# Encoder trunk on one core: weight sums issued by a budget, two small moves in the order

## The chip, the cores and the metric

The kernel runs on one core of a Trainium2 chip (trn2). The metric is the device time of one execution in microseconds. A core has TensorE (PE; its weight loads are shown apart as PEld), VectorE (DVE), ScalarE (ACT), GpSimd (POOL), and SyncE (SP), which here only issues DMAs.

## The reference

One layer of an encoder, batch 1, 512 tokens of width 1024, all float32:

```
x += [hgrn2 heads ; mlstm heads](rmsnorm(x) @ w_in + b_in) @ w_out
x += cross_attention(rmsnorm(x), rmsnorm(mem))       # 4 heads, 256 memory tokens: w_xq, w_xkv, w_xo
x += square(relu(rmsnorm(x) @ w_up)) @ w_down        # 1024 -> 4096 -> 1024
return rmsnorm(x)
```

Both groups of recurrent heads (four and four, of width 128) run a forward and a backward scan.

## The kernel before, in words

**Products.** Weights lie in DRAM as blocks of 128x1024 float32 (512 KB), in the order of use (`wpk`, `SEQ`). A block is loaded by SP into a tile `st` (three buffers), and split in two: ScalarE rounds it into `wh`, VectorE writes the rest, `st - wh`, into `wl` (`split_out`, L342; three buffers each). The activations are split in the same way. A product is then three matmuls per piece: high by high, high by low, low by high (L346 to L348, L1305 to L1307, L1588 to L1590). `weights` (L277) splits the block in use and the next two, and loads the fourth. So the split of block n writes over the buffers of block n-3, and waits until TensorE is done with that.

**Stages.** In this order: the input projection with the recurrent heads beside it (SEQ 0 to 36), K and V of the memory (37 to 52), the mixer's output projection (53 to 60), the query projection with the attention heads beside it (61 to 68), the cross-attention's output projection, and the MLP in four quarters of an up stage and a down stage each (st 0 to 7).

**Seven products for eight.** The cross-attention's output projection and the MLP's stages do a two by two block product with seven products, P1 to P7, each in two parts, a and b (`JOBS` L1161, `MORDER` L1215). P1 to P3 use plain weight blocks; P4 to P7 use sums of blocks, and activations that are sums too ("forms", made in `up`, L1540: `first` makes the P5 form, `second` the P6 form, `by_p3` and `by_p7` the others). The order of the MLP's products on TensorE is written out by hand.

**Sums of weights.** `make_forms` (L304) builds the MLP's weight sums in DRAM, beside the earlier stages: `start` and `follow` are plain copies issued by SP, `add` is an accumulating DMA issued by POOL. It is a generator of 88 steps, 44 copies and 44 adds of 512 KB each. `next_form` (L248) takes one step; a copy is put behind the last weight load in SP's order, an add waits for the last split that VectorE has made. `weights` takes a step for each block from SEQ 6 on, and a second one at every third (L283). That is 84 steps by the end of the query projection. The last four are taken in the MLP (L1280). The sums of the cross-attention's output projection are made in SBUF by other DMAs on POOL (`sum_loads`, `add_block` L1179; tiles `as` and `gate`); the MLP's down stages also add in SBUF (`sum_add`, tile `as`).

**The order elsewhere** is set by a scheduler that follows the program, with `tc.high_priority()` lifting what stands in it. In `up`, the weight splits and the readings of PSUM stand in it; the squares (`square`, L1545: ReLU, then square, on ScalarE) don't.

**The gates.** `gates_chain` (L708) makes the mLSTM decay terms: two scans on VectorE over the rows (L782, twice), two more that need a row mask (L786, twice; the mask is loaded at L768), and a subtraction (L813), after which ScalarE copies the result (L815).

Of the kernel before, what the change touches and what calls it, by code (L numbers as in the profile page):

```python
# [80 lines left out]
def trunk(ctx: ExitStack, tc: tile.TileContext, x, mem, wpk, vec, cst, lmask, rmask, rows, out):  # L81
    nc = tc.nc
# [18 lines left out]
    def smb():  # L101
        return pss.tile([P, 512], F32, tag="sm", name=nm("sm"))
# [39 lines left out]
    def behind(a, b):  # L142

        tc.add_manual_dep(a.ins, b.ins.name, mybir.DependencyInfo(mybir.DependencyClass.NoSync, mybir.DependencyReason.DATA),
                          reason="order of an engine")
# [99 lines left out]
    st_tiles, hl_tiles = {}, {}  # L245
    last_load, last_made = [None], [None]

    def next_form():  # L248

        o = next(form_steps, None)  # L250
        if o is not None:
            if o.ins.engine == mybir.EngineType.SP:
                behind(o, last_load[0])
            else:
                after(o, last_made[0])
                accs.append(o)
# [20 lines left out]
    def weights(key):  # L277
        i = SIDX[key]
        with (tc.high_priority() if i > 2 else ExitStack()):
            for n in range(i, i + 3):  # L280
                split(n)
            load(i + 3)
        for _ in range((i >= 6) + (i >= 6 and i % 3 == 0)):  # L283
            next_form()
        return hl_tiles[i]

    mforms = {}
# [52 lines left out]
    form_steps = make_forms()  # L340
# [367 lines left out]
    def gates_chain():  # L708
        grow = ml["grow"]
        ps = smb()  # L710
# [43 lines left out]
        yield  # L754

        lp = A4()
        gp.memset(lp[:, 0:512], 0.0)
        for dr in range(2):
            v.tensor_copy(ap(lp, dr * 32, [P, 4], [1, 4]), ap(lf, dr * 4, [8, 4], [1, 4]))
            v.tensor_copy(ap(lp, 64 + dr * 32, [P, 4], [1, 4]), igd(dr))  # L760
        ps = smb()
# [2 lines left out]
        lrow = grow[:, 512:1024]  # L764
        sc.activation(lrow[0:64, 0:512], ps[0:64, :], AF.Copy)
        sc.activation(grow[0:64, 0:512], ps[64:128, :], AF.Copy)
        rm = lp[:, 512:1024]
        nc.sync.dma_start(out=rm[0:64, 0:512], in_=rmask)  # L768
        yield
        fm = A4()  # L770
        Fr, mr = fm[:, 0:512], fm[:, 512:1024]
# [17 lines left out]
        ps = smb()  # L789
# [195 lines left out]
    for t in range(2):  # L985
# [8 lines left out]
        r, _ = rstd_of(ss, 1, D)  # L994
# [6 lines left out]
    for k in range(8):  # L1001
        ps = smb()
        for t in range(2):
            pe.transpose(ps[:, t * P:t * P + P], mt[t][:, k * P:k * P + P], ident)
        g = vc[:, V_MEM + k:V_MEM + k + 1]
# [155 lines left out]
    JOBS = [(p, g) for p in ("P1", "P7", "P2", "P5", "P6", "P3", "P4") for g in range(2)]  # L1161
# [112 lines left out]
    def mahead(n):  # L1274
        with tc.high_priority():
            for m in range(n, n + 3):
                msplit(m)
            for m in range(n + 3, n + 7):
                mload(m)
        if n % 2 and n >= len(JOBS):  # L1280
            next_form()
        return mhl[n]


# [5 lines left out]
    def by_blocks(st, sta, banks, done, ready=None, after=None):  # L1290

        mlp = st >= 0
        user = {"P1": 0, "P2": 1, "P5": 2, "P6": 0, "P3": 2, "P7": 0 if mlp else 3, "P4": 0}
        opens = {"P1", "P2", "P5"} if mlp else {"P1", "P2", "P5", "P7"}
        jobs = MORDER[st] if mlp else JOBS
        held = {}

        def product(p, g, u, w, first, end):
            for k in range(2):
                ah, al = [t[:, u * P:u * P + P] for t in sta[2 * g + k][p]]  # L1300
                bh, bl = [t[:, k * 512:k * 512 + 512] for t in w]
                new = first and k == 0 and p in opens
                fl = dict(skip_group_check=True)
                ps = held[user[p]][u]
                pe.matmul(ps, lhsT=ah, rhs=bh, start=new, stop=False, **fl)  # L1305
                pe.matmul(ps, lhsT=ah, rhs=bl, start=False, stop=False, **fl)  # L1306
                pe.matmul(ps, lhsT=al, rhs=bh, start=False, stop=end and k == 1, **fl)  # L1307
            if after is not None:
                after()

        def ahead(n):
            if mlp:
                return mahead(len(JOBS) * st + n)
            with tc.high_priority():
                for m in range(n, n + 3):
                    job(m)
                i = max(hl_tiles)
                for m in range(i + 1, i + 4):
                    load(m)
                for m in range(n + 3 - len(JOBS), n + 7 - len(JOBS)):  # L1320
                    if m >= 0:
                        mload(m)
            return job(n)

        def finished(p, u):
            for t0, c, sign in INTO[mlp][p]:
                done(t0 + u, c, held[user[p]][u], sign, (p, t0, c) in LAST[mlp])

        n = 0
        while n < len(jobs):  # L1330
            p, g = jobs[n]
            if ready is not None:
                ready(p, g)
            if user[p] not in held:
                held[user[p]] = banks[user[p]]()
            if p == "P4":
                ws = [ahead(n), ahead(n + 1)]
                for u in range(2):
                    for g in range(2):
                        product(p, g, u, ws[g], False, g == 1)  # L1340
                    finished(p, u)
                n += 2
                continue
            w = ahead(n)
            for u in range(2):
                product(p, g, u, w, g == 0, g == 1)
                if g == 1:
                    finished(p, u)
            n += 1
# [190 lines left out]
    def up(st):  # L1540

        A, B, C, y, forms = {}, {}, {}, {}, {}
        fl = dict(skip_group_check=True)

        def square(t, src):  # L1545
            sc.activation(t, src, AF.Relu)
            sc.activation(t, t, AF.Square)
# [6 lines left out]
        def first(g):  # L1554
            v.tensor_tensor(out=y[3, g], in0=y[2, g], in1=y[3, g], op=ALU.subtract)
            form("P5", g, y[3, g], A4)
# [15 lines left out]
        for n, (p, g) in enumerate(MORDER[st]):  # L1572
            hi, lo = mahead(len(JOBS) * st + n)
            if p == "P1":
                A[g] = smb()
            if p == "P2":
                B[g] = mmb()
            if p == "P5":
                C[g] = mmb()
            ps = B[g] if p == "P2" else C[g] if p in ("P5", "P3") else A[g]  # L1580
            xh, xl = xf[p]
            for k in range(2):
                o = ps[:, k * 256:k * 256 + 256]
                for kt in range(4):
                    z = slice(k * 512 + kt * P, k * 512 + kt * P + P)
                    m = slice(kt * 256, kt * 256 + 256)
                    new = k == kt == 0 and p in ("P1", "P2", "P5")
                    pe.matmul(o, lhsT=hi[:, z], rhs=xh[:, m], start=new, stop=False, **fl)  # L1588
                    pe.matmul(o, lhsT=hi[:, z], rhs=xl[:, m], start=False, stop=False, **fl)  # L1589
                    pe.matmul(o, lhsT=lo[:, z], rhs=xh[:, m], start=False, stop=kt == 3, **fl)  # L1590
                after_product()
            if p == "P1":
                y[0, g] = msum[g][:, 2048:2560]
                with tc.high_priority():
                    sc.activation(y[0, g], ps, AF.Copy)
            elif p == "P2":
                with tc.high_priority():
                    v.tensor_tensor(out=y[0, g], in0=y[0, g], in1=ps, op=ALU.add)
                square(y[0, g], y[0, g])
                form("P1", g, y[0, g], yt)  # L1600
            elif p == "P5":
                y[3, g] = T2()[:, 0:512]
                with tc.high_priority():
                    sc.activation(y[3, g], ps, AF.Copy)
            elif p == "P6":
                y[1, g] = rrow[:, (1 - g) * 512:(1 - g) * 512 + 512]
                with tc.high_priority():
                    sc.activation(y[1, g], ps, AF.Copy)
            if p in ("P3", "P6") and {("P3", g), ("P6", g)} <= set(MORDER[st][:n + 1]):
                z = y[1, g]  # L1610
                v.tensor_tensor(out=z, in0=C[g], in1=z, op=ALU.subtract)
                square(z, z)
                form("P2", g, z, G4)
                done.add(("P2", g))
                if ("P4", 0) in done and g == 0:
                    by_p3(0)
            if p == "P7":
                with tc.high_priority():
                    v.tensor_tensor(out=y[3, g], in0=y[3, g], in1=ps, op=ALU.subtract)
                square(y[3, g], y[3, g])  # L1620
                form("P4", g, y[3, g], A4)
            elif p == "P4":
                y[2, g] = T2()[:, 0:512]
                square(y[2, g], ps)
                with tc.high_priority():
                    first(g)
                done.add(("P4", g))
                if g == 0:
                    second(g)
                    by_p7(g)  # L1630
                    if ("P2", 0) in done:
                        by_p3(g)
# [118 lines left out]
```

## Time and profile before

| | us |
|---|---|
| three runs | 826.61, 830.08, 830.45 |
| median of the runs | 830.08 |
| the profiled execution | 828.69 |
| its span in the trace | 826.9 |
| TensorE busy | 804.2 |
| VectorE busy | 618.8 |
| ScalarE busy | 485.7 |
| GpSimd busy | 96.4 |

The span runs from the first to the last instruction of the trace; the profiled execution's own time has 1.8 us around it. The granted TensorE clock is full throughout. A matmul's end in the profile is modelled, and matmuls overlap, so the busy time is the time in which at least one is under way.

### The profile page before, as it was taken

To read this page: it belongs to the slowest core of one execution; us is meant where nothing else is said; L and a number is where in the kernel's file an instruction comes from. 1 tells how busy PE (TensorE), PEld (TensorE's weight loads), DVE (VectorE), ACT (ScalarE), POOL (GpSimd) and SP (SyncE) were. 2 spreads that over 40 slices of the span, in tenths; PEclk is the share of its full clock that TensorE was granted. 3 is DMA by queue.
4 is the path that set the end of the run, shared out by engine and by line. 5 is a ranking of instruction groups with operands and counts; after the bars stand their busy time and mean duration, and the time that the engine had idled before them with its cause. 6 is when DMAs were issued, how large, how long until landed. Compare 5 with 4: busy or idle time off the path is not lost.

```text
span 826.9 us, 14074 instructions
## 1 busy us (share of the span) xinstructions
PE 804.2 (97%) x5438; PEld 692.9 (84%) x5438; DVE 618.8 (75%) x1033; ACT 485.7 (59%) x854; POOL 96.4 (12%) x130
## 2 busy tenths in 40 slices
PE   8999999999999989999999999999999999999995
PEld 6787788887888978887888889987998899789974
DVE  6567975699479978555567979996589758875895
ACT  5247464445578475455445678863596458546854
POOL 2000021300220210321110001021001000100001
PEclk9999999999999999999999999999999999999999
DMA  7366478874893999998783355679966686768552
GB/s 277 118 239 204 150 173 210 208 227 104 192 279 124 242 337 279 262 200 262 189 232 79 89 126 182 203 206 278 300 207 157 207 277 201 193 200 252 170 153 102
DMA packets 56597, 167.26 MB, mean 202 GB/s; under 512 B 5393, under 2 KB 5521, under 8 KB 56530
## 3 DMA queue, kind: packets, MB, share of 16 engines
q1 hardware_dynamic: 41200, 126.04, 43.7%
q0 software_dynamic: 15040, 39.85, 26.6%
q8 instruction: 43, 0.70, 0.3%
q10 hardware_dynamic: 290, 0.47, 0.2%
q14 instruction: 24, 0.20, 0.1%
HBM read 164.24 MB, written 48.23 MB: 257 GB/s over the span
## 4 chain that ended last, share of the span: by engine, by line
PE 77%; DVE 9%; issue 4%; DMA 4%; ACT 4%; POOL 1%; POOLq 0%; ACTq 0%; DVEq 0%
PE mm L346 11%; PE mm L347 11%; PE mm L348 11%; PE sm L1307 4%; PE sm L1306 4%; PE sm L1305 4%; PE sm L1589 4%; PE sm L1590 4%; PE sm L1588 4%; DVE wl L343 3%; PE mm L1589 3%; PE mm L1590 3%; PE mm L1588 3%; DMA st<-in_wpk 3%; ACT wh L343 2%
## 5 line engine op out<-in xcount | busy, mean ns | idle before, releaser
L343 DVE TENSOR_TENSOR wl<-st,wh 128x1024 fp32r<-128x1024 f32 x165 | 201.5, 1223 | 108.7 <-ACT wh L343 105.0
L343 ACT ACTIVATE wh<-st 128x1024 fp32r<-128x1024 f32 x165 | 174.1, 1057 | 171.9 <-PE mm L347 44.1
L346 PE MATMUL mm<-xT,wh 128*128 128x512 f32 x288 | 115.6, 402 | 0.0
L348 PE MATMUL mm<-xT,wl 128*128 128x512 f32 x288 | 113.1, 393 | 0.1
L347 PE MATMUL mm<-xT,wh 128*128 128x512 f32 x288 | 112.8, 392 | 0.3 <-DVE xT L1060 0.3
L300 POOL DMA_DIRECT2D form_P<-in_wpk x44 | 45.6, 1106 | 321.4 <-DVE wl L343 264.5
L1307 PE MATMUL sm<-wh,a 128*128 128x512 f32 x180 | 70.5, 392 | 2.0 <-DVE a L343 2.0
L1305 PE MATMUL sm<-wh,a 128*128 128x512 f32 x180 | 70.5, 392 | 0.9 <-ACT wh L343 0.6
L1306 PE MATMUL sm<-wl,a 128*128 128x512 f32 x180 | 70.2, 390 | 0.8 <-DVE wl L343 0.8
L348 PEld LDWEIGHTS mm<-xT,wl 128*128 128x128 f32 x288 | 54.1, 188 | 11.8 <-DVE wl L343 0.3
L347 PEld LDWEIGHTS mm<-xT,wh 128*128 128x128 f32 x288 | 54.2, 188 | 11.0 <-DVE xT L1060 0.9
L346 PEld LDWEIGHTS mm<-xT,wh 128*128 128x128 f32 x288 | 54.1, 188 | 10.8 <-ACT wh L343 0.3
L300 POOL DMA_DIRECT2D as<-in_wpk x20 | 18.1, 940 | 226.6 <-DVE wl L343 131.1
L1307 PEld LDWEIGHTS sm<-wh,a 128*128 128x128 f32 x180 | 33.8, 188 | 10.5 <-DVE a L343 3.6
L1305 PEld LDWEIGHTS sm<-wh,a 128*128 128x128 f32 x180 | 33.8, 188 | 8.9 <-ACT wh L343 1.7
L1306 PEld LDWEIGHTS sm<-wl,a 128*128 128x128 f32 x180 | 33.8, 188 | 8.1 <-DVE wl L343 1.1
L1589 PE MATMUL sm<-yT,wh 128*128 128x256 f32 x128 | 36.3, 284 | 0.7 <-DVE yT L343 0.7
L1589 PE MATMUL sm<-xT,wh 128*128 128x256 f32 x128 | 36.4, 285 | 0.3 <-DVE xT L343 0.2
L1589 PE MATMUL mm<-xT,wh 128*128 128x256 f32 x128 | 36.3, 284 | 0.2 <-DVE xT L343 0.2
L1588 PE MATMUL sm<-xT,wh 128*128 128x256 f32 x128 | 36.4, 284 | 0.0
L1588 PE MATMUL mm<-xT,wh 128*128 128x256 f32 x128 | 36.3, 284 | 0.0
L1590 PE MATMUL sm<-yT,wl 128*128 128x256 f32 x128 | 36.2, 283 | 0.0
(388 smaller groups left out, 2111.6 us busy)
## 6 DMA issues: line engine op xcount, KB each, us to landing
st<-in_wpk SPq DMA_DIRECT2D x123, 512.0 KB, 4.2
form_P<-in_wpk POOLq DMA_DIRECT2D x44, 512.0 KB, 9.1
st<-form_P SPq DMA_DIRECT2D x42, 512.0 KB, 5.0
form_P<-in_wpk SPq DMA_DIRECT2D x26, 512.0 KB, 6.8
as<-in_wpk POOLq DMA_DIRECT2D x24, 512.0 KB, 9.0
form_P<-form_P SPq DMA_DIRECT2D x18, 512.0 KB, 6.9
gate<-in_wpk POOLq DMA_DIRECT2D x8, 512.0 KB, 5.6
as<-form_P SPq DMA_DIRECT2D x8, 512.0 KB, 5.7
```

The costliest lines, as they stand in the source:

```text
L300: return eng.dma_start(out=dst, in_=mblock(st, g, *b), max_dma_last_dim=4096, **kw)
L343: return sc.activation(dst_hi, src, AF.Copy), v.tensor_tensor(out=dst_lo, in0=src, in1=dst_hi.bitcast(F32), op=ALU.subtract)
L346: pe.matmul(ps, lhsT=ah, rhs=bh, start=first, stop=False)
L347: pe.matmul(ps, lhsT=ah, rhs=bl, start=False, stop=False)
L348: pe.matmul(ps, lhsT=al, rhs=bh, start=False, stop=last)
L1305: pe.matmul(ps, lhsT=ah, rhs=bh, start=new, stop=False, **fl)
L1306: pe.matmul(ps, lhsT=ah, rhs=bl, start=False, stop=False, **fl)
L1307: pe.matmul(ps, lhsT=al, rhs=bh, start=False, stop=end and k == 1, **fl)
L1588: pe.matmul(o, lhsT=hi[:, z], rhs=xh[:, m], start=new, stop=False, **fl)
L1589: pe.matmul(o, lhsT=hi[:, z], rhs=xl[:, m], start=False, stop=False, **fl)
L1590: pe.matmul(o, lhsT=lo[:, z], rhs=xh[:, m], start=False, stop=kt == 3, **fl)
```

## The change

It does three things.

- Steps of weight sums are taken by a budget: `allow(n)` adds n, and steps are taken while it is above zero; a copy costs 1, an add 2. A block from SEQ 6 on gives 2, but 1 in the projections of K and V; each product of the cross-attention's output projection gives 2.
- The row mask's load stands at the start of its part of `gates_chain`, at high priority.
- In `up`, the two ScalarE instructions that square the form of P4 stand at high priority.

```
-    def next_form():
-        o = next(form_steps, None)
-        if o is not None:
+    budget = [0]
+    def allow(n):
+        budget[0] += n
+        while budget[0] > 0:
+            o = next(form_steps, None)
+            if o is None:
+                return
+            budget[0] -= 1 if o.ins.engine == mybir.EngineType.SP else 2
             if o.ins.engine == mybir.EngineType.SP:
                 behind(o, last_load[0])
             else:
...
-        for _ in range((i >= 6) + (i >= 6 and i % 3 == 0)):
-            next_form()
+        allow(0 if i < 6 else 1 if key[1] == "kv" else 2)
...
         lp = A4()
+        rm = lp[:, 512:1024]
+        with tc.high_priority():
+            nc.sync.dma_start(out=rm[0:64, 0:512], in_=rmask)
...
-        rm = lp[:, 512:1024]
-        nc.sync.dma_start(out=rm[0:64, 0:512], in_=rmask)
...
-        if n % 2 and n >= len(JOBS):
-            next_form()
+        if n % 2:
+            allow(2)
...
             if mlp:
                 return mahead(len(JOBS) * st + n)
+            allow(2)
...
                 y[2, g] = T2()[:, 0:512]
-                square(y[2, g], ps)
                 with tc.high_priority():
+                    square(y[2, g], ps)
                     first(g)
```

Counted from the calls, the steps fall so:

| stage | copies and adds before | now |
|---|---|---|
| input projection | 24, 18 | 24, 19 |
| K and V of the memory | 11, 10 | 6, 5 |
| mixer's output projection | 3, 8 | 6, 5 |
| query projection | 6, 4 | 2, 7 |
| cross-attention's output projection | 0, 0 | 6, 8 |
| MLP | 0, 4 | 0, 0 |

The order of TensorE's instructions is the same. On VectorE, the second scan of L786 moves up to stand right behind the first, ahead of a weight split, and L813 moves ahead of L557. Three other places follow as the program orders them, before and now; line numbers of the change are 5 to 7 higher.

SP in the projections of K and V, from the load of block 43 (`st` from `in_wpk`) on; `form_P` from `in_wpk` is the copy that starts a sum. Before:

```order
L263 DMA st_3042<-in_wpk 128x1024
L263 DMA st_3094<-in_wpk 128x1024
L263 DMA st_3141<-in_wpk 128x1024
L300 DMA form_P_0_3144<-in_wpk 256x1x512
L300 DMA form_P_0_3151<-in_wpk 128x1024
L263 DMA st_3209<-in_wpk 128x1024
L300 DMA form_P_0_3156<-in_wpk 256x1x512
L263 DMA st_3267<-in_wpk 128x1024
L300 DMA form_P_1_3148<-in_wpk 256x1x512
```

and now:

```order
L269 DMA st_3041<-in_wpk 128x1024
L269 DMA st_3092<-in_wpk 128x1024
L269 DMA st_3139<-in_wpk 128x1024
L269 DMA st_3185<-in_wpk 128x1024
L269 DMA st_3243<-in_wpk 128x1024
L269 DMA st_3302<-in_wpk 128x1024
L269 DMA st_3337<-in_wpk 128x1024
L269 DMA st_3371<-in_wpk 128x1024
L305 DMA form_P_0_3374<-in_wpk 256x1x512
```

The first copy of the second half of the MLP's sums stood behind the load of block 45, and stands behind that of block 50.

ScalarE in the MLP's first down stage: `wh` from `st` or `as` are the splits of the weights of P5a, P5b, P6a and P6b in turn, `a_853` is the high half of the second P5 form (used by P5b), `a_849` that of a P3 form, `a_862` that of the second P6 form. Before:

```order
L343 ACTIVATE wh_5666<-st_5514 128x1024
L343 ACTIVATE a_844_5552<-as_5133 128x512
L343 ACTIVATE wh_5688<-st_5559 128x1024
L343 ACTIVATE a_849_5592<-rg_4666 128x512
L343 ACTIVATE a_853_5627<-t_823_5374 128x512
L343 ACTIVATE wh_5711<-as_5134 128x1024
L343 ACTIVATE wh_5731<-as_5134 128x1024
L343 ACTIVATE a_862_5685<-t_823_5374 128x512
```

and now:

```order
L348 ACTIVATE wh_5670<-st_5518 128x1024
L348 ACTIVATE a_844_5556<-as_5137 128x512
L348 ACTIVATE wh_5692<-st_5563 128x1024
L1553 ACTIVATE rg_4656<-rg_4656 128x512
L1554 ACTIVATE rg_4656<-rg_4656 128x512
L348 ACTIVATE wh_5714<-as_5138 128x1024
L348 ACTIVATE gate_5665<-rg_4656 128x512
L348 ACTIVATE wh_5734<-as_5138 128x1024
L348 ACTIVATE a_849_5596<-rg_4656 128x512
L348 ACTIVATE a_853_5631<-t_823_5378 128x512
L348 ACTIVATE a_862_5689<-t_823_5378 128x512
```

The two high halves stood ahead of the splits for P6a and P6b, and stand behind both; the squares and the split of a P2 form (`rg`, `gate`) have moved up. On VectorE the low halves of the two stand behind the split for P6b in the same way.

POOL in the cross-attention's output projection: `gate` are the adds that turn the weights of P7 into those of P6, and later those of P6 into those of P4; the two operations of L1439 belong to the norm ahead of the MLP. Before:

```order
L1181 DMA gate_4311<-in_wpk 128x1024
L1181 DMA gate_4312<-in_wpk 128x1024
L1181 DMA gate_4311<-in_wpk 128x1024
L1181 DMA gate_4312<-in_wpk 128x1024
L1439 TENSOR_TENSOR tiny_5046<-tiny_5043,misc 128x2
```

and now:

```order
L305 DMA form_P_0_3387<-in_wpk 256x1x512
L1187 DMA gate_4301<-in_wpk 128x1024
L1187 DMA gate_4302<-in_wpk 128x1024
L305 DMA form_P_1_3379<-in_wpk 256x1x512
L305 DMA form_P_1_3391<-in_wpk 256x1x512
L305 DMA form_P_0_3376<-in_wpk 256x1x512
L305 DMA form_P_0_3388<-in_wpk 256x1x512
L1187 DMA gate_4301<-in_wpk 128x1024
L1187 DMA gate_4302<-in_wpk 128x1024
L305 DMA form_P_1_3380<-in_wpk 256x1x512
L305 DMA form_P_1_3392<-in_wpk 256x1x512
L1446 TENSOR_TENSOR tiny_5050<-tiny_5047,misc 128x2
```

Eight adds of the MLP's sums (seven of them shown, with the pairs of `gate` between them) stand in this stretch, where there were none.

## Rows read from the trace of the kernel before

**Rows 1.** The page's busy times, share of the span and instructions, by engine.

```profile
PE 804.2 (97%) x5438; PEld 692.9 (84%) x5438; DVE 618.8 (75%) x1033; ACT 485.7 (59%) x854; POOL 96.4 (12%) x130
```

**Rows 2.** Waits of PE: who waited for whom, us in total, times, longest.

```profile
PE sm L1307 <- DVE a L343: 2.0, 3, 0.9
PE sm L878 <- ACT as L872: 1.5, 1, 1.5
...
PE sm L571 <- DVE t L558: 1.3, 1, 1.3
...
PE sm L686 <- DVE t L679: 1.1, 2, 0.6
...
PE sm L1306 <- DVE wl L343: 0.8, 1, 0.8
...
PE sm L1305 <- ACT wh L343: 0.6, 1, 0.6
```

**Rows 3.** Timeline, gates chain: start, us, instruction [idle before, releaser].

```profile
69.14 1.21 DVE L786 TENSOR_TENSOR_SCAN a<-a,a 4x512 f32<-4x512 f32 x1
70.38 0.69 DVE L557 TENSOR_TENSOR a<-t,a 128x512 f32<-128x512 f32 x1
70.99 0.68 DVE L813 TENSOR_TENSOR a<-a 64x512 f32<-64x512 f32 x1
...
71.70 0.63 ACT L815 ACTIVATE ar<-a 64x512 fp32r<-64x512 f32 x1 [3.73 <-DVE a L813]
```

**Rows 4.** Timeline of ACT in the projections of K and V.

```profile
295.28 1.06 ACT L343 ACTIVATE wh<-st 128x1024 fp32r<-128x1024 f32 x1 [1.37 <-DMA st<-in_wpk]
...
300.46 1.06 ACT L343 ACTIVATE wh<-st 128x1024 fp32r<-128x1024 f32 x1 [3.33 <-DMA st<-in_wpk]
```

**Rows 5.** DMA issues, 264 to 300 us: count, KB each, median us to landing.

```profile
form_P<-in_wpk SPq DMA_DIRECT2D x7, 512.0 KB, 13.7
form_P<-in_wpk POOLq DMA_DIRECT2D x6, 512.0 KB, 12.5
```

**Rows 6.** DMA issues, 545 to 575 us (first down stage).

```profile
form_P<-in_wpk POOLq DMA_DIRECT2D x4, 512.0 KB, 14.3
...
st<-in_wpk SPq DMA_DIRECT2D x4, 512.0 KB, 10.8
```

**Rows 7.** Timeline, first down stage, around the start of P5b.

```profile
544.04 0.62 ACT L343 ACTIVATE a<-t 128x512 fp32r<-128x512 f32 x1
...
545.72 1.22 DVE L343 TENSOR_TENSOR wl<-as,wh 128x1024 fp32r<-128x1024 f32 x1
...
546.85 0.68 DVE L343 TENSOR_TENSOR a<-t,a 128x512 fp32r<-128x512 f32 x1
...
547.11 0.39 PE L1305 MATMUL sm<-wh,a 128*128 128x512 f32 x1
...
547.34 0.39 PE L1306 MATMUL sm<-wl,a 128*128 128x512 f32 x1
547.36 1.06 ACT L343 ACTIVATE wh<-as 128x1024 fp32r<-128x1024 f32 x1 [1.71 <-PE sm L1307]
```

**Rows 8.** Timeline, third down stage, at P5b.

```profile
707.42 0.69 DVE L343 TENSOR_TENSOR a<-t,a 128x512 fp32r<-128x512 f32 x1
...
708.16 0.50 PE L1307 MATMUL sm<-wh,a 128*128 128x512 f32 x1 [0.93 <-DVE a L343]
```

**Rows 9.** Windows, ahead of it: us, busy of each engine, PEclk, DMA share, GB/s.

```profile
694.00:709.00 15.00, 14.07 (x80) 11.95 (x79) 15.00 (x21) 12.61 (x19) 0.88 (x1) 1.00 0.44 141
```

**Rows 10.** Timeline, cross-attention's output projection: last gate add, split of its block.

```profile
476.93 0.87 POOL L1181 DMA_DIRECT2D gate<-in_wpk  x1 [2.49 <-DVE wl L343]
...
485.29 1.06 ACT L343 ACTIVATE wh<-gate 128x1024 fp32r<-128x1024 f32 x1 [0.48 <-ACT t L1040]
```

**Rows 11.** Windows, the same projection.

```profile
440.00:490.00 50.00, 50.00 (x245) 41.94 (x244) 42.69 (x70) 29.28 (x54) 3.47 (x4) 1.00 0.42 95
```

**Rows 12.** DMA issues, 440 to 490 us.

```profile
gate<-in_wpk POOLq DMA_DIRECT2D x4, 512.0 KB, 5.5
```

## The prediction

> **What bounds the kernel.** The first view to read is the page's busy times: TensorE is busy for 804.2 of 826.9 us [rows 1], so at most about 23 us can be won without taking matmuls away, and the change takes none away. The order of TensorE's instructions is the same before and after, row for row. What can change is only when TensorE waits. So the second view is the list of its waits [rows 2]. Six of its lines matter here: one wait of 1.5 us (the mLSTM products at L878, for ScalarE), one of 1.3 us (scores at L571, for VectorE), two of 1.1 us together (L686), one each of 0.8 and 0.6 us (L1306 and L1305, for the halves of a weight block), and three of 2.0 us together (L1307, the third matmul of a down product, which needs the low half of an activation form). The third view is the timeline of ScalarE and VectorE just ahead of each wait; the fourth, the DMA issues of the same stretch, tells whether a late weight block lies behind it. For each part of the change I ask which of these waits it ends, and which it makes.
>
> The 0.5% that a measurement of this kernel can tell from no change is 4.15 us of the median 830.08: faster means under 825.93, slower over 834.23. The profiled execution took 828.69 us, 1.39 below that median; the sum is made against 828.69.
>
> **Sums out of the memory K and V projections.** With the change ten adds and eleven copies in these sixteen blocks become five and six, and the copies come only behind load fifty. Between 264 and 300 us the kernel before issued six adds from POOL, landing after a median of 12.5 us, and seven copies from SP, landing after 13.7 us [rows 5]. Two weight splits on ScalarE were held by late blocks there, for 1.37 and 3.33 us [rows 4]; the exponentials behind the second one came late, and TensorE waited 1.5 us for them at L878 [rows 2]. I take the whole wait: **-1.5 us**. Bounds: 0, if the blocks stay late, and -2.6, if the two waits at L686 shrink as well; I hold with the 1.5 because those two are released by VectorE [rows 2], not by a transfer. The steps taken out go to the mixer's output projection, the query projection and the cross-attention's output projection. I cost them at nothing; the cover is that in the last, from 440 to 490 us, the DMA share is 0.42 and TensorE is busy for all 50 us [rows 11]. What it costs if this cover is gone is the third rival.
>
> **Sums out of the first MLP stages.** The last four adds were issued between 545 and 575 us, into the first down stage. There they landed after a median of 14.3 us and the weight blocks beside them after 10.8 [rows 6]; for the two halves of a late block TensorE waited 0.6 and 0.8 us [rows 2]. With the change none of these adds is left in the MLP. **-1.4 us**; the bound on the other side is 0.
>
> **The row mask.** Its load goes out one place sooner on SP, ahead of a weight block that is split three blocks later, which costs nothing that anyone waits for. What moves is VectorE: the second decay scan (L786) now stands right behind the first, and the subtraction of L813 comes ahead of L557. L557 held it from 70.38 to 70.99, and ScalarE sat idle for 3.73 us until L813 was done, with a weight split and the projection's evacuations behind it [rows 3]; these lead to TensorE's 1.3 us wait at L571 [rows 2]. L813 comes sooner by those 0.61 us. I take **-0.5 us**; bounds 0 (a projection ends too late for ScalarE to use it) and -1.3 (the whole wait). The weight split on VectorE that now stands behind the second scan comes 1.21 us later [rows 3], which costs nothing: a block is split three blocks ahead.
>
> **The squares of the fourth form.** In the down stages of the second, third and fourth quarter, ScalarE now squares P4 sooner, and VectorE makes the difference of L1555 one weight split sooner. But what TensorE waits for is the low half of the form made from it, and in VectorE's order that still stands behind the same instructions: it starts at 707.42, and TensorE's matmul at 708.16 after 0.93 us [rows 8]. VectorE is busy for all 15 us from 694 to 709 [rows 9]; the same work in another order ends at the same time. So **0 us**; bounds -2.0 (all three waits of that line end) and 0.
>
> In the first quarter it does something else. ScalarE's new order puts the split of the weights of P6b ahead of the two high halves a_849 and a_853; before, both halves stood ahead of it. This split writes over the buffer of P5a, so it waits until TensorE is done with P5a, and a_853 is the operand of P5b, the very next product. In the trace of before the high half was made from 544.04 on, its low half from 546.85 on, P5b started at 547.11, and that split at 547.36 after 1.71 us of idling for TensorE [rows 7]. In the new order, from 547.36: the split takes 1.06, each high half 0.62, so a_853's is there at 549.66. VectorE needs 1.13 for the low half of the weights (545.72 to 546.85), from 548.42, so it is free at 549.55 and writes a_853's low half from 549.66 to 550.34 (0.68). P5b then starts at 549.66 instead of 547.11, and its third matmul at 550.34, where two steps of 0.23 (547.11 to 547.34) would have put it at 550.12: 2.55 + 0.22, about **+2.7 us**. Bounds: +2.0, should the instructions overlap by some tenths each, and +3.3, if a_849 in turn waits for VectorE. Next in line is P6b's form: two products of 2.76 us (twelve steps) stand ahead of it, and VectorE has some six instructions for it, about 4 us, so it is in time.
>
> [...] The trace shows ScalarE idle for 1.71 us behind a split that waits [rows 7], and for 3.73 us behind a copy that waits, with ready work behind it [rows 3]. [...]
>
> **Sum.** -1.5 - 1.4 - 0.5 + 0 + 2.7 = -0.7, so 828.69 - 0.7 = **828.0 us**: no change that can be told.
>
> **Rivals.** *First: the relief without the new wait.* The splits' order costs nothing, because ScalarE gets past the split in time: 828.69 - 3.4 = 825.3. Against it stands the idle 1.71 us, which ended with P5a's end and not sooner [rows 7]. Chance 0.15.
>
> *Second: the squares do help.* The three waits at L1307 end (2.0 us) and the wait at P5b comes: 828.0 - 2.0 = 826.0. For it: the square is what L1555 needs. Against it: VectorE has no gap into which the low half could move up [rows 8, 9]. Chance 0.10.
>
> *Third, on the other side: the sums collide in the cross-attention's output projection.* Eight adds and six copies now run there, and POOL's order puts form adds ahead of the adds (tile gate) that finish the weights of P6 and P4. Such a gate add landed after 5.5 us [rows 12]; the last was issued at 476.93, and the split of its block began at 485.29 [rows 10]. The split is made two products ahead, 5.5 us, and takes 1.06 and 1.22 us for its halves [rows 7], so it has 3.2 us to spare. TensorE waits once that add takes over 11.6 us (485.29 + 3.2 - 476.93). At the 14.3 us that adds took in the first down stage [rows 6] it waits 2.7, and the time is 830.7; at 18 us it would be 834.4. For it: fourteen more transfers of 512 KB in one stretch. Against it: the share of 0.42 [rows 11], and that the first four adds need nothing from the stretch itself. [...] Chance 0.10.
>
> *Fourth: no relief.* The weight blocks stay late in both stretches, since the steps only moved next door: 828.69 - 0.5 + 2.7 = 830.9. Chance 0.05.
>
> **How the numbers follow.** The forecast holds 0.60. The low ends of its terms (-2.6, -1.4, -1.3, -2.0, +2.0) seldom meet; without any of the gains the high end is 828.69 + 3.3 = 832.0. The first two rivals lie at 825.3 and 826.0, the third and fourth above 830. The runs of before spread over 826.61 to 830.45, and I add some of that on either side: 823.5 to 832.5. Faster: most of the first rival, a third of the second, and a little of the forecast, 0.22. Slower by over 0.5%: the upper half of the third and little else, 0.07. Same: 0.71.
>
> **What would show it.** Right: ScalarE's copy at L815 starts some 0.5 us sooner; no split held by a block for over 1 us between 264 and 300 us, and no wait of TensorE at L878; none for a weight block in the first down stage; a new wait of TensorE of 2 to 3 us at P5b's first matmul there, put down to ScalarE's form; the waits of 0.9 us in the later down stages still there. Wrong: no wait at that P5b (first rival), the 0.9 us gone (second), TensorE waiting for weights of P4 near 488 us (third), splits still held (fourth).

## The result, and the profile after

Twenty runs of the changed kernel gave a median of 833.02 us (829.31 to 835.96), twenty of the kernel before 827.92 (825.62 to 830.45). The ratio is 1.006, with an interval of 1.0045 to 1.0075: slower by 0.6%. The forecast was 828.0, "no change that can be told", in a range up to 832.5; slower had a chance of 0.07.

The profiled execution took 833.50 us, 4.8 more than that of before. The page's busy times and the waits of PE answer to [rows 1] and [rows 2]:

```profile
PE 808.2 (97%) x5438; PEld 696.1 (84%) x5438; DVE 619.1 (74%) x1033; ACT 485.7 (58%) x854; POOL 95.4 (11%) x130
```

```profile
PE sm L1423 <- DVE vv L1397: 2.6, 1, 2.6
PE sm L1311 <- ACT a L348: 2.2, 1, 2.2
PE sm L1313 <- DVE a L348: 1.5, 2, 1.1
...
PE mm L1312 <- DVE wl L348: 0.8, 1, 0.8
...
PE sm L576 <- DVE t L563: 0.7, 1, 0.7
...
PE mm L1311 <- ACT wh L348: 0.4, 1, 0.4
```

Three things are gone or smaller: the wait at L878 (1.5), those for the weights of the first down stage (0.6 and 0.8), and half of the one for VectorE's t (1.3, now 0.7). Four are new, in two places. The wait of 2.2 us at L1311 is P5b of the first down stage, as forecast. The other three, at L1311, L1312 (both into mm) and L1423, lie together in the cross-attention's output projection. TensorE's timeline of the changed kernel there:

```profile
486.52 0.49 PE L1311 MATMUL mm<-wh,yT 128*128 128x512 f32 x1 [0.40 <-ACT wh L348]
487.78 0.50 PE L1312 MATMUL mm<-wl,yT 128*128 128x512 f32 x1 [0.76 <-DVE wl L348]
...
491.81 1.50 PE L1423 MATMUL sm<-cs,vv 128*128 128x128 f32 x4 [2.60 <-DVE vv L1397]
```

They come to 3.8 us. ScalarE and VectorE ahead of them, and the last two gate adds on POOL:

```profile
485.41 1.06 ACT L348 ACTIVATE wh<-gate 128x1024 fp32r<-128x1024 f32 x1 [7.17 <-DMA gate<-in_wpk]
...
488.84 1.06 ACT L348 ACTIVATE wh<-gate 128x1024 fp32r<-128x1024 f32 x1 [1.15 <-DMA gate<-in_wpk]
```

```profile
469.38 1.22 DVE L348 TENSOR_TENSOR wl<-gate,wh 128x1024 fp32r<-128x1024 f32 x1
...
489.93 1.23 DVE L348 TENSOR_TENSOR wl<-gate,wh 128x1024 fp32r<-128x1024 f32 x1 [1.61 <-ACT wh L348]
491.07 1.28 DVE L1397 TENSOR_TENSOR vv<-vv,sm 128x512 f32<-128x512 f32 x2
```

```profile
473.62 1.03 POOL L305 DMA_DIRECT2D form_P<-in_wpk  x1 [6.76 <-DMA form_P<-form_P]
474.18 2.32 POOL L1187 DMA_DIRECT2D gate<-in_wpk  x2
```

The two adds were issued at 474.18 and 474.7. They landed after 11.1 and 14.0 us, at 485.3 and 488.7, and the splits started then. Behind the second split stands the residual's sum `vv` on VectorE, and TensorE's next instructions want that: hence the 2.6 us.

The first add was late twice over. The split that frees its buffer had ended at 470.60 (469.38 + 1.22), but ahead of it in POOL's order stood a form add that waited for a copy until 473.62. In early_budget, below, where no form add stands there, the same split ended at 470.95 and the gate add was issued at 471.24. So about 3.3 us of its lateness are POOL's order (an estimate from these rows), and 11.1 in place of some 5.5 us are the landing. The second add was held in POOL's order by about half a microsecond; its lateness is the landing. The DMA issues of 470 to 490 us, and the windows (us, busy of each engine, PEclk, DMA share, GB/s), answer to [rows 11, 12]:

```profile
form_P<-in_wpk POOLq DMA_DIRECT2D x3, 512.0 KB, 15.3
gate<-in_wpk POOLq DMA_DIRECT2D x2, 512.0 KB, 12.6
st<-in_wpk SPq DMA_DIRECT2D x2, 512.0 KB, 13.1
```

```profile
440.00:490.00 50.00, 48.05 (x233) 39.62 (x231) 36.93 (x63) 26.43 (x48) 10.34 (x11) 1.00 0.98 218
...
470.00:490.00 20.00, 18.05 (x85) 14.20 (x84) 10.92 (x16) 9.35 (x19) 5.00 (x5) 1.00 1.03 228
```

The share that was 0.42 is 0.98, and the last two gate adds take 12.6 us at the median, where such adds took 5.5. Then the column of the granted clock, which stood at 1.00 in the whole trace of before up to TensorE's last instruction:

```profile
490.00:492.00 2.00, 0.19 (x1) 0.18 (x1) 2.00 (x3) 1.06 (x2) 0.00 (x0) 0.93 1.12 223
492.00:494.00 2.00, 1.88 (x9) 1.60 (x9) 1.73 (x4) 2.00 (x7) 0.15 (x1) 0.50 0.65 120
494.00:496.00 2.00, 2.00 (x8) 1.57 (x8) 0.00 (x0) 2.00 (x6) 0.56 (x1) 0.72 0.61 153
550.00:552.00 2.00, 0.51 (x3) 0.08 (x1) 1.82 (x4) 1.46 (x2) 0.93 (x1) 1.00 0.88 332
552.00:554.00 2.00, 1.31 (x3) 0.79 (x4) 2.00 (x4) 0.64 (x2) 0.85 (x2) 0.79 1.06 217
554.00:556.00 2.00, 2.00 (x6) 1.52 (x6) 1.04 (x3) 0.63 (x1) 0.92 (x2) 0.50 1.07 207
556.00:558.00 2.00, 2.00 (x9) 1.60 (x8) 1.99 (x4) 0.47 (x1) 0.00 (x0) 0.86 1.07 207
```

Behind each of the two places with new waits the granted clock stands at 0.50 while TensorE is at work again: from 492.0 to 495.0 us and from 553.5 to 556.5 in every window of 0.5 us. Behind the second, matmuls of 512 columns start 0.42 to 0.43 us apart (554.11 to 556.24), where they start 0.23 us apart ahead of the wait (549.21 to 549.44). What that costs is estimated as the missing share times the window: (0.07 + 0.50 + 0.28) x 2 = 1.7 us behind the first, (0.21 + 0.50 + 0.14) x 2 = 1.7 us behind the second.

Added up, the profile pays 3.8 + 2.2 + 1.7 + 1.7 = 9.4 us and gets back 1.5 (L878) + 1.4 (first down stage) + 0.6 (L576) + 0.5 (the low half at L1307, 2.0, now 1.5 at L1313) + 1.4 (a wait for the first loads of the program, which differs between the traces: 0.2 us in squares_alone, 2.9 in early_budget_squares_back) = 5.4. The difference of 4.0 is most of the 4.8. The last of these terms stood in the kernel before as:

```profile
PE sm L434 <- DMA cs<-in_cst: 1.4, 1, 1.4
```

TensorE's own sums agree: its time without work rose by only 0.8 us (22.7 to 23.5 of the span), its busy time, for the same matmuls, by 4.0.

### The profile page after: what moved, and what is told of

It reads as the page before. It is cut to its first block, busy times and chain, and to the rows that moved or that the text cites. A ratio compares the mean times of both kernels' runs of the same rounds, so it can differ in the third digit from the quotient of the medians.

```text
span 831.7 us, 14078 instructions
## 1 busy us (share of the span) xinstructions
PE 808.2 (97%) x5438; PEld 696.1 (84%) x5438; DVE 619.1 (74%) x1033; ACT 485.7 (58%) x854; POOL 95.4 (11%) x130
## 4 chain that ended last, share of the span: by engine, by line
PE 77%; DVE 11%; DMA 5%; issue 3%; ACT 2%; POOL 1%; POOLq 0%; SPq 0%; DVEq 0%; ACTq 0%
PE mm L351 11%; PE mm L353 11%; PE mm L352 11%; PE sm L1313 4%; PE sm L1596 4%; PE sm L1311 4%; PE sm L1597 4%; PE sm L1312 4%; PE sm L1595 4%; DVE wl L348 3%; PE mm L1596 3%; PE mm L1597 3%; PE mm L1595 3%; DMA form_P<-form_P 2%; DMA gate<-in_wpk 2%
## 5 line engine op out<-in xcount | busy, mean ns | idle before, releaser
L1311 PE MATMUL sm<-wh,a 128*128 128x512 f32 x180 | 70.8, 394 | 2.4 <-ACT a L348 2.2
L1313 PE MATMUL sm<-wh,a 128*128 128x512 f32 x180 | 71.3, 396 | 1.6 <-DVE a L348 1.5
L1312 PE MATMUL sm<-wl,a 128*128 128x512 f32 x180 | 70.7, 393 | 0.0
L1313 PEld LDWEIGHTS sm<-wh,a 128*128 128x128 f32 x180 | 34.2, 190 | 10.4 <-DVE a L348 3.4
L1311 PEld LDWEIGHTS sm<-wh,a 128*128 128x128 f32 x180 | 34.2, 190 | 10.2 <-ACT a L348 2.6
L1312 PEld LDWEIGHTS sm<-wl,a 128*128 128x128 f32 x180 | 34.1, 189 | 7.2
L348 ACT ACTIVATE wh<-as 128x1024 fp32r<-128x1024 f32 x24 | 25.4, 1057 | 19.8 <-PE sm L1313 12.0
```

The lines of the kernel that those rows point to most:

```text
L348: return sc.activation(dst_hi, src, AF.Copy), v.tensor_tensor(out=dst_lo, in0=src, in1=dst_hi.bitcast(F32), op=ALU.subtract)
```

## The experiments

The theory after this reading: two new waits, each with a fall of the clock behind it, hide a relief that is real. The first four kernels take them apart.

**squares_back**: the squares as in the kernel before, all else as changed.

```
-                with tc.high_priority():
-                    square(y[2, g], ps)
+                square(y[2, g], ps)
+                with tc.high_priority():
                     first(g)
```

> The changed kernel with the squares of P4 back at normal priority; the budget and the row mask stay. Theory: the time that the change costs comes from two new waits of TensorE, in the cross-attention's output projection (3.8 us) and ahead of P5b of the first down stage (2.2 us), and each is followed by some 3.4 us at a granted clock of 0.50, which costs another 1.7 us. Without the moved squares the wait ahead of P5b and its fall of the clock are both gone: 2.2 + 1.7 = 3.9 us less than the changed kernel's 833.5, so 829.6; the clock stays 1.00 from 545 to 565 us, and the waits of the projection stay. Rival 1: the fall of the clock there has another cause and stays; then 831.3. Rival 2: the wait ahead of P5b only covered the late weights of P3a (1.4 us of waits in the kernel before), which come back; then 831.0.

Measured: 830.05 us (827.45 to 831.61), 1.002 of before (1.0007 to 1.0033), 3.0 us less than the changed kernel. The wait ahead of P5b is gone and the clock is full there; the waits in the output projection and the fall behind them stay:

```profile
540.00:550.00 10.00, 10.00 (x56) 8.69 (x55) 9.96 (x14) 7.77 (x11) 0.00 (x0) 1.00 0.54 168
550.00:560.00 10.00, 10.00 (x45) 8.05 (x44) 9.82 (x14) 6.22 (x9) 2.70 (x3) 1.00 0.95 217
490.00:492.00 2.00, 0.25 (x1) 0.14 (x1) 2.00 (x3) 1.06 (x2) 0.00 (x0) 1.00 1.13 239
492.00:494.00 2.00, 1.73 (x9) 1.65 (x9) 1.67 (x4) 2.00 (x7) 0.21 (x1) 0.61 0.81 151
494.00:496.00 2.00, 2.00 (x7) 1.58 (x6) 0.00 (x0) 1.98 (x6) 0.51 (x1) 0.54 0.74 159
```

The late weights of P3a (the 0.6 and 0.8 us in the first down stage of the kernel before) did not come back in this trace.

**early_budget**: no budget in the output projection, a larger one early in the first stage.

```
-        allow(0 if i < 6 else 1 if key[1] == "kv" else 2)
+        allow(0 if i < 6 else 1 if key[1] == "kv" else 3 if i < 28 else 2)
...
-            allow(2)
             with tc.high_priority():
                 for m in range(n, n + 3):
                     job(m)
```

> The changed kernel with the squares at high priority as they are, but no budget in the cross-attention's output projection, and 3 in place of 2 for the weights 6 to 27 of the first stage, so that all sums are made before that projection. Theory: the adds that finish the weights of P6 and P4 there landed after 11.1 and 14.0 us because eight adds and six copies ran beside them; alone they land after some 5.5 us as in the kernel before, no wait is left from 484 to 495 us, the clock stays 1.00 there, and the time falls by 3.8 + 1.7 = 5.5 us to 828.0; the wait ahead of P5b stays. Rival 1: those adds are late by their place in POOL's order and not by the other transfers; then they land no sooner, 833.5. Rival 2: the sums put into the first stage delay weights there; a new wait in the first 200 us, 829 to 832.

Measured: 828.53 us (825.96 to 829.17), 1.000 of before (0.9989 to 1.0012), 4.5 less than the changed kernel. Its gate adds, and the window of 470 to 490 us:

```profile
469.73 1.22 DVE L348 TENSOR_TENSOR wl<-gate,wh 128x1024 fp32r<-128x1024 f32 x1
471.24 0.87 POOL L1187 DMA_DIRECT2D gate<-in_wpk  x1 [19.55 <-DVE wl L348]
```

```profile
gate<-in_wpk POOLq DMA_DIRECT2D x2, 512.0 KB, 5.4
```

```profile
470.00:490.00 20.00, 20.00 (x102) 16.62 (x101) 15.10 (x21) 13.94 (x29) 2.45 (x3) 1.00 0.52 112
```

The gate adds land after 5.4 us and TensorE is busy for all 20 us. This run takes the form adds out of POOL's order as well as out of the DMA engines, so it doesn't tell what each of the two is worth. The fourteen steps that went from the output projection to the earlier stages made no new wait there. The wait ahead of P5b (2.2 us) and the fall of the clock behind it are there unchanged:

```profile
548.00:550.00 2.00, 2.00 (x5) 1.61 (x6) 1.12 (x2) 0.63 (x1) 1.37 (x2) 0.50 1.02 199
```

**early_budget_squares_back**: both edits.

> Both edits: all sums made before the output projection, and the squares of P4 at normal priority. Theory: the costs are independent, both waits and both falls of the clock are gone, the relief of the weights' loads at 300 and 567 us is kept: 833.5 - 5.5 - 3.9 = 824.1, about 0.5% less than the kernel before. Rival: the late weights of P3a (1.4 us) come back, or the first stage has new waits; then 825.5 to 828.

Measured: 823.93 us (822.63 to 826.52), 0.9947 of before (0.9928 to 0.9965). Both costs gone, the relief is left: 9.1 us less than the changed kernel. Alone the two edits gave 3.0 and 4.5, so together they gave 1.6 more than their sum; the interval of this run is about 1.5 us to either side, and no run shows whether there is more to it. One thing of the rival did show: a wait of 0.8 us for P3a's weights is back in this trace.

**filled_wait**: what the fall of the clock hangs on. The changed kernel, with 18 matmuls more where TensorE waits ahead of P5b.

```
+            if st == 1 and (p, g) == ("P5", 0):
+                lt, rt_ = (t[:, 0:P] for t in sta[0]["P1"]), sta[0]["P1"][1]
+                lt = next(lt)
+                for _ in range(18):
+                    pe.matmul(held[user[p]][0][:, 0:256], lhsT=lt, rhs=rt_, start=False, stop=False, skip_group_check=True)
             n += 1
```

> The changed kernel with 18 more products of 256 columns (2.2 us by their cadence of 0.12 us) ahead of P5b in the first down stage, where TensorE waits 2.2 us; they take operands that are long there, no other engine's order changes, and their products are added to the sum of P5, which changes the output. Theory: the granted clock falls because TensorE stood still; with the wait filled P5b starts at about the same time, the clock stays 1.00 from 552 to 560 us, and the time is 1.7 us less than the changed kernel's 833.5: 831.8. Rival: the clock falls there for another reason (the load of DMA, what DVE and ACT do); it falls to 0.50 all the same and the time is 833.5 or more.

Measured: 831.00 us (828.73 to 832.59), 1.0033 of before (1.0018 to 1.0049): 2.0 us less than the changed kernel (whose interval, 1.0045 to 1.0075, overlaps this one a little), with 18 matmuls more. TensorE's timeline, then the windows:

```profile
549.69 2.31 PE L1360 MATMUL sm<-yT 128*128 128x256 f32 x18
552.05 0.50 PE L1311 MATMUL sm<-wh,a 128*128 128x512 f32 x1
```

```profile
550.00:552.00 2.00, 2.00 (x17) 1.80 (x15) 1.83 (x3) 2.00 (x3) 0.85 (x1) 1.00 1.06 383
552.00:554.00 2.00, 1.87 (x8) 1.25 (x8) 2.00 (x4) 0.00 (x0) 1.49 (x2) 1.00 1.01 190
554.00:556.00 2.00, 2.00 (x11) 1.65 (x10) 1.92 (x5) 1.17 (x2) 0.27 (x1) 1.00 1.00 190
```

P5b starts when its form is ready, as in the changed kernel, and the clock stays full, with a DMA share of 1.00 to 1.06 and VectorE no less busy than there. So the load around it did not make the clock fall in this execution; what it lacks against the changed kernel is TensorE's standing still. By the times, 2.0 us less, the fall has a price of its own.

**squares_alone**: the kernel before with the squares at high priority (the opposite of the first diff).

> The kernel before with the squares of P4 at high priority and nothing else. Theory: TensorE waits 2.2 us ahead of P5b of the first down stage and runs some 3.4 us at 0.50 behind that (1.7 us more); the late weights of P3a come by the transfers' time and not by TensorE's, so their two waits (1.4 us of the kernel before) are covered by the new one: 827.9 + 2.2 + 1.7 - 1.4 = 830.4. Rival 1: nothing is covered, since P3a's load is issued later too; then 831.8. Rival 2: the wait needs the transfers that the budget moved out of the stage, and is absent here; then 827.9.

Measured: 829.21 us (827.96 to 831.02), 1.0006 of before (0.9997 to 1.0015, which holds no change at all), 1.0 us more by the medians. A miss. Its waits, and the windows at P5b:

```profile
PE sm L1305 <- ACT a L343: 2.2, 1, 2.2
...
PE sm L1306 <- DVE wl L343: 1.2, 2, 0.8
PE sm L1307 <- DVE a L343: 1.2, 1, 1.2
```

```profile
548.00:550.00 2.00, 0.26 (x1) 0.26 (x2) 1.82 (x3) 1.69 (x3) 0.48 (x1) 1.00 1.03 367
550.00:552.00 2.00, 1.91 (x8) 1.25 (x8) 1.91 (x4) 0.26 (x1) 1.80 (x2) 1.00 0.92 119
552.00:554.00 2.00, 2.00 (x10) 1.64 (x10) 2.00 (x4) 1.21 (x2) 0.16 (x1) 1.00 1.04 178
```

The wait of 2.2 us is there, but no fall of the clock behind it. And the late weights of P3a (two waits, 1.2 us) are not covered by it, against the theory. So a wait of this length is not followed by a fall each time. Why this execution got by without one is not shown, nor whether the other eleven did.

**half_budget_squares_back**: squares as before, and `allow(1)` in place of `allow(2)` in the output projection.

> The changed kernel with the squares of P4 at normal priority and a budget of 1 in place of 2 in each call of the output projection; the steps left over are taken in the MLP. It stands against squares_back (830.05) and early_budget_squares_back (823.9). Theory: the lateness of the adds that finish P6's and P4's weights is a matter of how many transfers run beside them; at half the rate they land between the 5.5 us that they took alone and the 11.1 to 14.0 us of the changed kernel, some 9 us; the waits in the projection shrink from 3.8 to under 1.5 us, the granted clock stays 1.00, and the time is 824 to 826.5. Rival: one add in flight beside them is enough to make them late; then the waits and the fall of the clock stay, 829 to 830.5.

Measured: 826.59 us (825.53 to 828.53), 0.9986 of before (0.9975 to 0.9996), 3.5 us less than squares_back. The DMA issues of 470 to 490 us:

```profile
form_P<-form_P SPq DMA_DIRECT2D x3, 512.0 KB, 6.4
gate<-in_wpk POOLq DMA_DIRECT2D x2, 512.0 KB, 5.3
```

The gate adds are as quick as alone, quicker than expected. They were issued at 471.22 and 474.57; the three form adds of this stretch had landed by 472 us, and of the three copies only the first (476.84) went out before the last gate add had landed. So steps in this stage did no harm here by being there: what made the gate adds late was steps in flight with them, or ahead of them in POOL's order. The time is just over the 826.5 that the theory allowed, and 2.7 more than early_budget_squares_back. The steps left over were taken in the MLP; in its first up stage TensorE waits 2.3 us for `yT` here and 0.7 us in early_budget_squares_back. Whether those steps make that wait, and what the rest of the 2.7 is, is not shown.

**row_mask_alone**: the kernel before with the mask's load moved.

```
         lp = A4()
+        rm = lp[:, 512:1024]
+        with tc.high_priority():
+            nc.sync.dma_start(out=rm[0:64, 0:512], in_=rmask)
...
-        rm = lp[:, 512:1024]
-        nc.sync.dma_start(out=rm[0:64, 0:512], in_=rmask)
```

> The kernel before with the row mask loaded sooner and nothing else. Theory: TensorE's wait at 83 us falls from 1.3 to 0.7 us and no other wait changes, so the profile shows about 0.6 us less, below what the times can show. Rival: the load put ahead on SP delays the loads of weights behind it, and a wait appears between 70 and 100 us.

Measured: 827.36 us in one run. TensorE's wait there is 0.7 us, in place of 1.3:

```profile
PE sm L571 <- DVE t L558: 0.7, 1, 0.7
```

No wait appeared around it. The wait of 1.5 us at L878 was 0.8 us here (L879 in this kernel); that one varies by itself.

**early_budget_squares_late**: the squares at high priority in all down stages but the first.

```
+                with (tc.high_priority() if st > 1 else ExitStack()):
+                    square(y[2, g], ps)
                 with tc.high_priority():
-                    square(y[2, g], ps)
                     first(g)
```

> As early_budget_squares_back (823.9), but the squares of P4 stand at normal priority in the first down stage alone, and at high priority in the other three. Theory: in these the wait ahead of P5b is for the low half on VectorE, which is full there, and the moved squares put the split of the weights of P6b ahead of it: the waits at 707 and 787 us are 0.8 and 1.1 us as in early_budget, in place of 0.7 us in three waits, without a fall of the clock; 824.5 to 825.5, slower than with all squares at normal priority by about a us. Rival: the forecast's term, that the moved squares change nothing there; then 823.9.

Measured: 823.15 us (822.56 to 824.55), 0.994 of before (0.9927 to 0.9953). The theory of the expectation fell: the waits at 707 and 787 us were not there at all, so the moved squares don't make them. To see whether they end them, both kernels ran once more, side by side.

> The kernel of early_budget_squares_back once more, beside the next one on the same chip: all squares at normal priority. If the moved squares change nothing in the second, third and fourth down stage (the forecast's term) the two agree within their intervals; if they help there, this one is slower by 0.5 to 1 us.

> The kernel of early_budget_squares_late once more: squares at normal priority in the first down stage alone. By the two runs so far (823.93 and 823.15) it is 0.8 us less than all_back_again; by the forecast's term it is the same. Both stay near 0.9945 of the kernel before.

Measured: 823.56 us (0.9946, 0.9927 to 0.9964) with all squares at normal priority, 823.94 (0.9952, 0.9934 to 0.9969) with those of the later stages moved up. The order of the two turned round: no difference. The low half of P5b's form was waited for in both, 1.3 us in three waits and 0.9 in two.

## Why the prediction was wrong

**The step that failed** is the sentence on the steps that were taken out of the projections of K and V: "I cost them at nothing; the cover is that in the last, from 440 to 490 us, the DMA share is 0.42". The cover was not there. The fourteen steps moved into this stage took the share from 0.42 to 0.98 and the last two gate adds from 5.5 us to 11.1 and 14.0. That is the third rival, with its mechanism, its place and nearly its landing time (14.3), but with a chance of 0.10. What it held against itself was the mean over 50 us. That mean was made without the work that was to go there, and it says nothing of when the steps come: a form add waits on POOL for a copy or a split (6.76 us for a copy ahead of the one at 473.62, 2.20 for a split ahead of the one at 479.79), and so three of the adds came between 473 and 480 us, around the gate adds. The rival named POOL's order, but priced only the landing; the first gate add lost 3.3 us to the order as well. That the steps in this stage are the cause is shown by the kernel without that budget (4.5 us less) and by the one with half of it; how the 3.8 us divide between order and landing is not.

**The rival's price** was too small in two terms. It let one add be late; two were, and the three waits come to 3.8 us where it had 2.7. And neither it nor the forecast had a term for the clock. Each wait was priced as its own length, but by the estimate above 1.7 us more were paid behind each place in the profiled execution: 3.4 of the 9.4 us. The other executions point the same way. The median of the runs' mean granted clock is 0.993 for the changed kernel, 0.995 for squares_back and for early_budget, and 0.997 for early_budget_squares_back and for the kernel before that ran beside it; 0.002 of 830 us is 1.7 us (an estimate from these medians).

**The wait at P5b** was right in place, cause and size: 2.7 forecast (its own terms, 2.55 + 0.22, make 2.8), 2.2 measured, within the bounds of 2.0 to 3.3 (the instructions overlap by a tenth or so each). ScalarE's timeline in the changed kernel answers to [rows 7]:

```profile
550.54 1.06 ACT L348 ACTIVATE wh<-as 128x1024 fp32r<-128x1024 f32 x1 [1.04 <-PE sm L1313]
551.51 0.61 ACT L348 ACTIVATE a<-rg 128x512 fp32r<-128x512 f32 x1
552.02 0.61 ACT L348 ACTIVATE a<-t 128x512 fp32r<-128x512 f32 x1
```

The split that waits for P5a's end stands first, after 1.04 us of idling, the two high halves behind it, and P5b starts at 552.69. That ScalarE would not get past the split was the forecast's reading of the idle times in [rows 3] and [rows 7]; here it did not. Taking the squares back took the wait away, with 3.0 us (alone) or 4.6 (with the early budget, 828.53 to 823.93). Moving them in the kernel before cost only 1.0.

**The relief** came as forecast. Projections of K and V: -1.5 forecast; the wait at L878 is gone in the changed kernel, and no split is held by a block from 264 to 300 us. The transfers there, to set beside [rows 5]:

```profile
st<-in_wpk SPq DMA_DIRECT2D x8, 512.0 KB, 4.2
form_P<-in_wpk POOLq DMA_DIRECT2D x4, 512.0 KB, 7.4
```

The wait is there in all three traces without the budget (1.5, 1.4 and 0.8 us) and in none of the nine with it, so that it ends is the budget's doing; its size before was no constant. First down stage: -1.4 forecast, gone in the changed kernel. The three traces without the budget have 1.2 to 1.4 us of these waits, eight of the nine with it none; early_budget_squares_back has 0.8, and all_back_again, the same kernel, none. Whether TensorE's own lateness in the changed kernel gave the loads time there is not shown. Row mask: -0.5 forecast, -0.6 measured, with the whole change and by itself.

**The squares in the later stages**: 0 forecast, and 0 within the intervals of the two pairs of kernels.

**The other rivals** were wrong as whole cases. The forecast's terms but for the two that failed are found again in early_budget_squares_back: without the new waits the first rival's 825.3 was to be expected, 3.4 less than its base; measured were 3.9 less than the kernel before (827.78 to 823.93, in runs beside each other).

## What to carry to other kernels

A mean DMA share of 0.42 was no cover here for transfers that were moved into the stretch: it became 0.98, and the last two gate adds landed after 11.1 and 14.0 us in place of 5.5. Add the share of what is moved to the mean, and look at which deadline transfer (here an add that a weight split waits for) will have them beside it, or ahead of it in the order of the engine that issues it. Price a new wait of TensorE of some microseconds with what may follow at a lower granted clock, as well as with its length: by the estimate above 1.7 us at 0.50 behind either place of the changed kernel, nothing in squares_alone, where the clock stayed at 1.00 behind a wait of 2.2 us. The kernel that makes the sums in the first stage and leaves the squares where they were beats both kernels, by 0.5% against the one before.

## What had not been expected of the hardware

A wait of 2.2 us was followed by an estimated 1.7 us of loss at a granted clock of 0.50, and with independent matmuls in the wait (2.31 us of them) the clock stayed at 1.00 and the kernel was faster by 2.0 us. The same wait was followed by a fall in early_budget and by none in squares_alone; the waits in the output projection were followed by one in each of the three traces that have them (the changed kernel, squares_back, filled_wait). And the changed kernel's runs spread more than those of before (6.7 us against 4.8) with the mean granted clock going from 0.995 in the five shortest to 0.990 in the longest.
